# The second parts of the third mixer's weights, formed in the second feed-forward and kept in DRAM

## The chip, the core and the metric

The kernel runs on one NeuronCore of a Trainium2 chip. The metric is the device time of one execution in microseconds (us). The engines are TensorE (PE; its weight loads are PEld), VectorE (DVE), ScalarE (ACT), GpSimd (POOL) and SyncE (SP), which issues the DMAs of this kernel. Each works through its own instructions in the order in which they stand in the program, and waits on semaphores for the others.

## The reference

`x` is 512 tokens of 1024 features in float32. `first_block` is a feed-forward (SwiGLU of width 2816), a mixer (a gated linear recurrence beside a neighbourhood attention) and another feed-forward. `second_block` has two layers, each a mixer and a feed-forward with a convolution; the mixer of the second layer, the third mixer of the kernel, is the one concerned:

```python
def odd_mixer(h, w_in, w_out, w_cc, b_cc, ln_g, ln_b):
    p = h @ w_in
    a, gate, q, k, v = jnp.split(p, [...], axis=-1)
    g = a * jax.nn.sigmoid(gate)
    g = causal_dwconv(g, w_cc) + b_cc
    y_c = jax.nn.silu(layer_norm(g, ln_g, ln_b))
    y_d = stick_breaking(heads(q), heads(k), heads(v))
    return jnp.concatenate([y_c, y_d], axis=-1) @ w_out
```

`w_in` is 1024x2560 and `w_out` 1024x1024; the convolution has 31 taps over 512 channels, and the attention 8 heads of width 64.

## The kernel before

**Products in three parts.** Every float32 matrix is split into two float32r parts: `hi`, a rounded copy, and `lo = x - hi`. A product is three matmuls, hi·hi, lo·hi and hi·lo (`mm3`, lines 134 to 136). An activation is split by `split` (L128 on ACT, L129 on DVE), a weight tile by `wload`.

**Loading weights.** `wload` (L95) takes one tile of 128x1024 numbers (512 KB): a DMA from SP into one of three buffers `raw` (L104), a cast on ACT into one of three `whi` (L118), a subtraction on DVE into one of three `wlo` (L119). The three `raw` buffers are used in turn by all loads of the program; a buffer is free when its subtraction is done. `whi` and `wlo` are free when PE has used them. Some stages bring further buffers for their first loads (`bh`, `bl`), and the last projections of a mixer have `oh`, `ol`.

**Stages.** `build` goes through f1, m1, f2, e, f3, o, f4 (feed-forwards and mixers by turns). A stage's first projections are done by `begin` in two halves of 256 tokens, because the normalised activations `hh`, `hl` of the first half are there before those of the second. Ahead of the second half stands a chain on DVE, ACT and PE: the sums of squares, `rnorm` (L257 to L267), the new residual and its norm.

**The second feed-forward, f2** (`ffn`). For each of 22 `j` two projections of 24 matmuls of 512 columns, on weight tiles 2j and 2j+1, then a few operations on DVE and ACT (gate, product, split). Its 44 up tiles are the `raw<-w_ffn_gu` in the rows.

**The third mixer, o** (`odd`). It has 20 tiles of `w_in_odd` and 8 of `w_out_odd`. Generators for the projections and attention heads (`unit`, `gated`, `attend`) and for the convolution (`conv`, L1016 to L1020, 27 taps per channel group on DVE, 3 on ACT and POOL) are interleaved by `weave`. An attention head goes from PE (logits) to ACT (L970, L971), to DVE (a scan `f`, L973, and a product `b`, L974), to PE (transposes, L471), to ACT and DVE (L474, L475) and back to PE (L487).

The order of the instructions on each engine is set by the framework's scheduler when the kernel is built, and is fixed then.

Of the kernel before, what the change touches and what calls it, by code (L numbers as in the profile page):

```python
# [9 lines left out]
F32 = mybir.dt.float32  # L10
F32R = mybir.dt.float32r
AF = mybir.ActivationFunctionType
ALU = mybir.AluOpType
# [3 lines left out]
P = 128  # L17
S = 512
# [3 lines left out]
KF = DFF // P  # L22
# [9 lines left out]

HALVES = (slice(0, S // 2), slice(S // 2, S))
WHOLE = slice(0, S)


class Net:
# [56 lines left out]
    def wload(self, src, alloc=None, cuts=None):  # L94


        nc = self.nc
        n = math.prod(src.shape[1:])
        raw = self.wp.tile([P, 1024], F32, name="raw", tag="raw", bufs=3)
        if cuts is None:  # L100
            dst = raw[:, :n]
            if len(src.shape) == 3:
                dst = dst.rearrange("p (m k) -> p m k", m=src.shape[1])
            nc.sync.dma_start(dst, src)  # L104
        if alloc is None:
            his = [self.wp.tile([P, 1024], F32R, name="whi", tag="whi", bufs=3)[:, :n]]
            los = [self.wp.tile([P, 1024], F32R, name="wlo", tag="wlo", bufs=3)[:, :n]]
        else:
            his, los = alloc()
        if cuts is not None:  # L110
            his, los = ([t[:, a:b] for a, b in zip((0,) + cuts, cuts)] for t in (his[0], los[0]))
        out, c0 = [], 0
        for hi, lo in zip(his, los):
            c = slice(c0, c0 + hi.shape[1])
            if cuts is not None:
                nc.sync.dma_start(raw[:, c], src[:, c])
                self.load_x(HALVES[0], c0 // P, c.stop // P)
            nc.scalar.copy(hi, raw[:, c])  # L118
            nc.vector.tensor_tensor(out=lo, in0=raw[:, c], in1=hi.bitcast(F32), op=ALU.subtract)  # L119
            out += [(hi[:, f : f + P], lo[:, f : f + P]) for f in range(0, hi.shape[1], P)]  # L120
            c0 = c.stop
        return out

    def split(self, pool, src, tag, name="sp", bufs=None, eng=None):
        nc = self.nc
        hi = pool.tile([P, S], F32R, name=name + "h", tag=tag, bufs=bufs)
        lo = pool.tile([P, S], F32R, name=name + "l", tag=tag, bufs=bufs)
        nc.scalar.copy(hi, src)  # L128
        (eng or nc.vector).tensor_tensor(out=lo, in0=src, in1=hi.bitcast(F32), op=ALU.subtract)  # L129
        return hi, lo  # L130
# [12 lines left out]
    def proj(self, src, acts, kind="m", key=None):  # L143
# [5 lines left out]
        for k0 in range(0, K, 8):  # L149
            ks = range(k0, min(K, k0 + 8))  # L150
            w = self.wload(src[:, k0 * P : ks.stop * P])
            ks = self.order or ks
            self.mmk(ps, w, acts, ks, WHOLE, ks[0] if self.order else 0, ks[-1] if self.order else K - 1)
        return ps
# [22 lines left out]
    def finish(self, src, acts, split, evac, after, pool=None):  # L177
# [4 lines left out]
        for m in range(n):  # L182
            evac(m, self.proj(src[m], acts, "mo"[m % 2], key=("out", m)), WHOLE)
        if not split:
            return after(WHOLE)
        alloc = None
# [130 lines left out]
    def first_prep(self, spec):  # L317
# [3 lines left out]
        for k in range(KD):  # L321
            self.h_scaled(spec, k, WHOLE)
        for k in range(KD):
            self.stat(self.X[k], WHOLE, k == 0)

# [32 lines left out]
    def first_begin(self, tiles, allocs):  # L358
# [13 lines left out]
        def after():  # L372
            self.consts()
            for k in range(KD):
                self.stat(self.X[k], WHOLE, k == 0)
            self.prep(spec, WHOLE)
# [2 lines left out]
        self.begin(tiles, allocs, before, after, lambda: scaled(HALVES[0]))  # L379


    def ffn(self, up, down, nxt, conv=None, post=None):
        nc, tc = self.nc, self.tc
        with tc.tile_pool(name="mida", bufs=KD) as sa, tc.tile_pool(name="mid", bufs=2 * KF - KD) as sp:
            with tc.tile_pool(name="ft", bufs=2) as fp:
                part = lambda nm: [sp.tile([P, S], F32R, name=nm, tag="s") for _ in range(2)]
                tiles = [((up.tensor.name, i), up[i]) for i in range(6)]
                allocs = [lambda: (part("bh"), part("bl"))] * 3
                if self.early:
                    self.begin(tiles, allocs)  # L390
                else:
                    self.first_begin(tiles, allocs)
                    self.early = True
                R = self.R
                if conv is not None:
                    pads = [fp.tile([P, S + 2], F32, name=f"pad{i}", bufs=1) for i in range(2)]
                    for t in pads:
                        nc.gpsimd.memset(t[:, 0:2], 0.0)
                mids = []
                h = self.H  # L400
                for j in range(KF):
                    pg = self.proj(up[2 * j], h, "m", key=(up.tensor.name, 2 * j))
                    pu = self.proj(up[2 * j + 1], h, "o", key=(up.tensor.name, 2 * j + 1))
                    gp = fp.tile([P, S], F32, name="gp", tag="gp")
                    if conv is None:
                        nc.vector.tensor_tensor(out=gp, in0=pg, in1=R, op=ALU.mult)
                    else:
                        wn, bn, l = conv
                        pad = pads[j % 2]
                        nc.vector.tensor_tensor(out=pad[:, 2:], in0=pg, in1=R, op=ALU.mult)  # L410
                        w = lambda t: self.vec(wn, (l * 3 + t) * KF + j)
                        nc.scalar.activation(gp, pad[:, 2:], AF.Identity, bias=self.vec(bn, l * KF + j), scale=w(2))
                        nc.vector.scalar_tensor_tensor(gp, pad[:, 1 : S + 1], w(1), gp, ALU.mult, ALU.add)
                        nc.vector.scalar_tensor_tensor(gp, pad[:, 0:S], w(0), gp, ALU.mult, ALU.add)
                    nc.scalar.activation(gp, gp, AF.Silu)
                    md = fp.tile([P, S], F32, name="md", tag="md")
                    nc.vector.tensor_tensor(out=md, in0=pu, in1=gp, op=ALU.mult)  # L417
                    mids.append(self.split(sa if j < KD // 2 else sp, md, "s", "m"))
            with tc.tile_pool(name="fm", bufs=KD) as mp:
                mix = {}  # L420

                def evac(m, ps, c, last=False):
                    if post is None:
                        t = self.tmp("dx")
                        nc.vector.scalar_tensor_tensor(t[:, c], ps, 0.5, R[:, c], ALU.mult, ALU.mult)
                        nc.vector.tensor_tensor(out=self.X[m][:, c], in0=self.X[m][:, c], in1=t[:, c], op=ALU.add)
                        self.updated(nxt, m, c, last)
                    else:
                        if m not in mix:
                            mix[m] = mp.tile([P, S], F32, name="mix", tag="mix")  # L430
                        nc.vector.tensor_tensor(out=mix[m][:, c], in0=ps, in1=R[:, c], op=ALU.mult)
                        self.stat(mix[m], c, m == 0, "mix", last)

                def after(c):
                    if post is not None:
                        self.post(mix, *post, nxt, c)
                    self.prep(nxt, c)

                self.finish(down, mids, 3 if nxt[0] == "normed" else 2, evac, after)
# [676 lines left out]
def build(tc, ins, out, stages=STAGES):  # L1116
    with ExitStack() as ctx:
        n = Net(ctx, tc, ins)
        n.out = out
        n.early = stages[0] != "f1"  # L1120
        if n.early:
            n.consts()
        if n.early:
            n.first_prep(PREP[stages[0]])
            n.prep(PREP[stages[0]], WHOLE)
        for s, t in zip(stages, [*stages[1:], "end"]):
            nxt = PREP.get(t, ("end",))
            if s == "f1":
                n.ffn(ins["w_ffn1_gu"], ins["w_ffn1_down"], nxt)
            elif s == "m1":  # L1130
                n.mixer1(nxt)
            elif s == "f2":
                n.ffn(ins["w_ffn2_gu"], ins["w_ffn2_down"], nxt)
            elif s == "e":
                n.even(nxt)
            elif s == "f3":
                n.ffn(ins["w_up0"], ins["w_down0"], nxt, conv=("w_fc", "b_fc", 0), post=("norm_g", 3 * KD))
            elif s == "o":
                n.odd(nxt)
            elif s == "f4":  # L1140
                n.ffn(ins["w_up1"], ins["w_down1"], nxt, conv=("w_fc", "b_fc", 1), post=("norm_g", 7 * KD))
# [139 lines left out]
```

## Time and profile before

| | us |
|---|---|
| median of 3 runs | 2491.81 (2491.55 to 2491.85) |
| the profiled execution, its time | 2491.55 |
| its span | 2489.8 |
| PE busy | 2411.6 |
| DVE busy | 1470.8 |
| ACT busy | 1100.2 |
| mean granted clock of PE, share of full speed | 0.985 |

The span goes from the first instruction to the last and is what the rows' times count from; 1.75 us of the profiled execution's time lie around it. Busy times of one engine don't overlap with each other. A busy PE isn't one at its peak, since its matmuls are pipelined and each is shown longer than its share. In the timeline the second feed-forward's up phase goes from about 878 to 1117 us, and the third mixer from about 1829 to 2074.

### The profile page before, as it was taken

The numbers are of one execution on the slowest core, as the hardware profiler recorded it, in microseconds if no ns is written. First come the engines' busy times: TensorE is split into PE (matmuls) and PEld (weight loads), VectorE is DVE, ScalarE is ACT, GpSimd is POOL, SyncE is SP. The second block draws the span as 40 slices with busy tenths as digits, with TensorE's granted clock in tenths as the row PEclk, the third lists the DMA queues.
The fourth block names the chain that finished last, engine by engine and source line by source line (L and its number), as shares of the span: only waits on it lengthen the run. The fifth ranks groups of instructions, "written<-read, shape, count | busy, mean of one in ns | idle before, by whom it ended". The sixth has DMA issues, their size and how long they took to land.

```text
span 2489.8 us, 31983 instructions
## 1 busy us (share of the span) xinstructions
PE 2411.6 (97%) x12710; PEld 2056.2 (83%) x12710; DVE 1470.8 (59%) x2496; ACT 1100.2 (44%) x1793; POOL 39.8 (2%) x75
## 2 busy tenths in 40 slices
PE   9999999999999999999999999999998879999998
PEld 8888898777777798888987898888887759888887
DVE  5444357888888643433566665554369996655434
ACT  5222236766666532322456543333245656433322
POOL 0000000000000000000000000000001120000000
PEclk9999999999999999999999999999998989999999
DMA  4232333222322223233432322233331202223332
GB/s 149 94 101 91 95 112 124 94 80 86 99 79 91 89 89 101 94 97 94 133 107 81 106 77 68 93 102 88 117 105 61 68 26 94 68 94 100 91 95 93
DMA packets 70949, 232.03 MB, mean 93 GB/s; under 512 B 7984, under 2 KB 12720, under 8 KB 70800
## 3 DMA queue, kind: packets, MB, share of 16 engines
q1 hardware_dynamic: 70800, 229.99, 29.1%
q8 instruction: 100, 1.64, 0.3%
q14 instruction: 49, 0.40, 0.1%
HBM read 227.84 MB, written 2.12 MB: 92 GB/s over the span
## 4 chain that ended last, share of the span: by engine, by line
PE 83%; DVE 10%; ACT 4%; issue 1%; DMA 1%; POOL 0%; SPq 0%; ACTq 0%; DVEq 0%; POOLq 0%
PE psm L136 15%; PE psm L134 15%; PE psm L135 15%; PE pso L134 10%; PE pso L135 10%; PE pso L136 10%; DVE wlo L119 1%; ACT whi L118 1%; PE pst L471 1%; PE pso L487 1%; DVE pso L1018 1%; DVE f L973 1%; PE pst L136 1%; PE pst L134 1%; PE pst L135 1%
## 5 line engine op out<-in xcount | busy, mean ns | idle before, releaser
L118 ACT CAST whi<-raw 128x1024 fp32r<-128x1024 f32 (+3 forms) x402 | 408.5, 1017 | 835.0 <-issue 457.5
L119 DVE TENSOR_TENSOR wlo<-raw,whi 128x1024 fp32r<-128x1024 f32 (+3 forms) x402 | 474.8, 1182 | 312.2 <-ACT whi L118 310.8
L134 PE MATMUL psm<-hh,whi 128*128 128x512 f32 (+1 forms) x1512 | 572.0, 379 | 7.3 <-ACT hh L285 3.1
L136 PE MATMUL psm<-hl,whi 128*128 128x512 f32 (+1 forms) x1512 | 568.2, 376 | 0.1
L135 PE MATMUL psm<-hh,wlo 128*128 128x512 f32 (+1 forms) x1512 | 568.1, 376 | 0.0
L134 PEld LDWEIGHTS psm<-hh,whi 128*128 128x128 f32 x1512 | 285.0, 189 | 57.0 <-ACT hh L285 3.9
L136 PEld LDWEIGHTS psm<-hl,whi 128*128 128x128 f32 x1512 | 285.2, 189 | 50.1 <-DVE hl L286 1.1
L135 PEld LDWEIGHTS psm<-hh,wlo 128*128 128x128 f32 x1512 | 285.4, 189 | 46.4
L134 PE MATMUL pso<-hh,whi 128*128 128x512 f32 (+1 forms) x728 | 273.0, 375 | 0.9 <-ACT whi L118 0.9
L135 PE MATMUL pso<-hh,wlo 128*128 128x512 f32 (+1 forms) x728 | 272.7, 375 | 0.7 <-DVE wlo L119 0.7
L136 PE MATMUL pso<-hl,whi 128*128 128x512 f32 (+1 forms) x728 | 272.8, 375 | 0.0
L135 PE MATMUL psm<-mh,wlo 128*128 128x512 f32 (+1 forms) x506 | 172.4, 341 | 1.6 <-DVE wlo L119 1.6
L134 PE MATMUL psm<-mh,whi 128*128 128x512 f32 (+1 forms) x506 | 172.1, 340 | 0.0
L136 PE MATMUL psm<-ml,whi 128*128 128x512 f32 (+1 forms) x506 | 171.9, 340 | 0.0
L417 DVE TENSOR_TENSOR md<-pso,gp 128x512 f32<-128x512 f32 x84 | 58.1, 692 | 187.5 <-PE pso L136 186.0
L135 PEld LDWEIGHTS pso<-hh,wlo 128*128 128x128 f32 x728 | 138.2, 190 | 25.1 <-DVE wlo L119 1.0
L134 PEld LDWEIGHTS pso<-hh,whi 128*128 128x128 f32 x728 | 138.1, 190 | 24.8 <-ACT whi L118 1.1
L136 PEld LDWEIGHTS pso<-hl,whi 128*128 128x128 f32 x728 | 138.1, 190 | 24.6 <-issue 0.5
L135 PE MATMUL pso<-mh,wlo 128*128 128x256 f32 (+1 forms) x440 | 145.6, 331 | 1.3 <-DVE wlo L119 1.3
L134 PE MATMUL pso<-mh,whi 128*128 128x256 f32 (+1 forms) x440 | 145.8, 331 | 0.3 <-ACT whi L118 0.3
L136 PE MATMUL pso<-ml,whi 128*128 128x256 f32 (+1 forms) x440 | 145.7, 331 | 0.0
L135 PEld LDWEIGHTS psm<-mh,wlo 128*128 128x128 f32 x506 | 96.7, 191 | 12.8 <-DVE wlo L119 2.2
(291 smaller groups left out, 3729.9 us busy)
## 6 DMA issues: line engine op xcount, KB each, us to landing
raw<-w_up SPq DMA_DIRECT2D x88, 512.0 KB, 3.3
raw<-w_ffn_gu SPq DMA_DIRECT2D x87, 512.0 KB, 3.2
raw<-w_in SPq DMA_DIRECT2D x56, 512.0 KB, 3.3
raw<-w_ffn_down SPq DMA_DIRECT2D x40, 512.0 KB, 3.5
raw<-w_down SPq DMA_DIRECT2D x38, 512.0 KB, 3.5
raw<-w_in_even SPq DMA_DIRECT2D x24, 512.0 KB, 3.5
raw<-w_in_odd SPq DMA_DIRECT2D x20, 512.0 KB, 3.3
raw<-w_ffn_down SPq DMA_DIRECT2D x20, 384.0 KB, 3.1
```

The lines of the kernel that those rows point to most:

```text
L118: nc.scalar.copy(hi, raw[:, c])
L119: nc.vector.tensor_tensor(out=lo, in0=raw[:, c], in1=hi.bitcast(F32), op=ALU.subtract)
L134: nc.tensor.matmul(out, w[0], x[0], start=start, stop=False)
L135: nc.tensor.matmul(out, w[1], x[0], start=False, stop=False)
L136: nc.tensor.matmul(out, w[0], x[1], start=False, stop=stop)
L417: nc.vector.tensor_tensor(out=md, in0=pu, in1=gp, op=ALU.mult)
L471: nc.tensor.transpose(pt[:, i * P : (i + 1) * P], p[:, i * P : (i + 1) * P], self.ident)
L487: nc.tensor.matmul(o[:, q0:q1], V[:, g, a].rearrange("p i d -> p (i d)"), p[:, c], start=first, stop=g == 3 and p is pl, skip_group_check= ...
L973: nc.vector.tensor_tensor_scan(r, r, zero.to_broadcast([P, w]), 1.0, ALU.mult, ALU.add)
L1018: nc.vector.scalar_tensor_tensor(t, pad[:, i : i + S], w(i), t, ALU.mult, ALU.add)
```

## The change

A new class `Split` stands for a weight tensor with its second part in DRAM. `presplit` walks over the tiles of a weight: it loads one into a `raw` buffer, casts its halves to a temporary `hi` on ACT, subtracts in place on DVE, so that `raw` holds the second part, and writes `raw` to DRAM. It is a generator; `ffn` of f2 takes 28 steps of it, spread over the 22 `j` of the up phase (20 tiles of `w_in_odd`, then 8 of `w_out_odd`). `wload` of such a tensor loads the tile into `raw` and casts it to `hi` as before, and brings the second part by a DMA into `wlo`, `bl` or `ol` where the subtraction was.

```diff
--- before.py
+++ after.py
@@ -32,6 +32,19 @@
 
 HALVES = (slice(0, S // 2), slice(S // 2, S))
 WHOLE = slice(0, S)
+
+
+class Split:
+
+
+    def __init__(self, raw, lo):
+        self.raw, self.lo, self.shape = raw, lo, raw.shape
+
+    def __getitem__(self, i):
+        return Split(self.raw[i], self.lo[i])
+
+    def rearrange(self, *a, **kw):
+        return Split(self.raw.rearrange(*a, **kw), self.lo.rearrange(*a, **kw))
 
 
 class Net:
@@ -96,6 +109,7 @@
 
         nc = self.nc
         n = math.prod(src.shape[1:])
+        src, second = (src.raw, src.lo) if isinstance(src, Split) else (src, None)
         raw = self.wp.tile([P, 1024], F32, name="raw", tag="raw", bufs=3)
         if cuts is None:
             dst = raw[:, :n]
@@ -116,10 +130,32 @@
                 nc.sync.dma_start(raw[:, c], src[:, c])
                 self.load_x(HALVES[0], c0 // P, c.stop // P)
             nc.scalar.copy(hi, raw[:, c])
-            nc.vector.tensor_tensor(out=lo, in0=raw[:, c], in1=hi.bitcast(F32), op=ALU.subtract)
+            if second is not None:
+                dst = lo
+                if len(src.shape) == 3:
+                    dst = dst.rearrange("p (m k) -> p m k", m=src.shape[1])
+                nc.sync.dma_start(dst.bitcast(F32), second)
+            else:
+                nc.vector.tensor_tensor(out=lo, in0=raw[:, c], in1=hi.bitcast(F32), op=ALU.subtract)
             out += [(hi[:, f : f + P], lo[:, f : f + P]) for f in range(0, hi.shape[1], P)]
             c0 = c.stop
         return out
+
+    def presplit(self, name):
+
+        nc, src = self.nc, self.ins[name]
+        lo = self.dp.tile(list(src.shape), F32, name=name + "_lo")
+        self.ins[name] = Split(src, lo)
+        for m in range(src.shape[0]):
+            raw = self.wp.tile([P, 1024], F32, name="raw", tag="raw", bufs=3)
+            nc.sync.dma_start(raw, src[m])
+            low = raw.bitcast(F32R)
+            for c in (slice(0, S), slice(S, 2 * S)):
+                hi = self.tmp("hi", dt=F32R)
+                nc.scalar.copy(hi, raw[:, c])
+                nc.vector.tensor_tensor(out=low[:, c], in0=raw[:, c], in1=hi.bitcast(F32), op=ALU.subtract)
+            nc.sync.dma_start(lo[m], raw)
+            yield
 
     def split(self, pool, src, tag, name="sp", bufs=None, eng=None):
         nc = self.nc
@@ -379,7 +415,7 @@
         self.begin(tiles, allocs, before, after, lambda: scaled(HALVES[0]))
 
 
-    def ffn(self, up, down, nxt, conv=None, post=None):
+    def ffn(self, up, down, nxt, conv=None, post=None, extra=None):
         nc, tc = self.nc, self.tc
         with tc.tile_pool(name="mida", bufs=KD) as sa, tc.tile_pool(name="mid", bufs=2 * KF - KD) as sp:
             with tc.tile_pool(name="ft", bufs=2) as fp:
@@ -416,6 +452,10 @@
                     md = fp.tile([P, S], F32, name="md", tag="md")
                     nc.vector.tensor_tensor(out=md, in0=pu, in1=gp, op=ALU.mult)
                     mids.append(self.split(sa if j < KD // 2 else sp, md, "s", "m"))
+                    if extra is not None:
+                        gen, steps = extra
+                        for _ in range(steps * (j + 1) // KF - steps * j // KF):
+                            next(gen, None)
             with tc.tile_pool(name="fm", bufs=KD) as mp:
                 mix = {}
 
@@ -1130,7 +1170,10 @@
             elif s == "m1":
                 n.mixer1(nxt)
             elif s == "f2":
-                n.ffn(ins["w_ffn2_gu"], ins["w_ffn2_down"], nxt)
+                extra = n.chain(n.presplit("w_in_odd"), n.presplit("w_out_odd"))
+                n.ffn(ins["w_ffn2_gu"], ins["w_ffn2_down"], nxt, extra=(extra, 28))
+                for _ in extra:
+                    pass
             elif s == "e":
                 n.even(nxt)
             elif s == "f3":
```

How the instructions stand. Line numbers behind "now" are those of the changed file: L118 is the load into `raw`, L137 that of the second part, L151 and L157 the load and the write of `presplit`.

SP, in the middle of f2's up phase, now (before, these are loads `raw<-w_ffn_gu` alone, 44 in a row):

```order
L118 DMA raw<-w_ffn_gu 128x1024
L151 DMA raw<-w_in_odd 128x1024
L118 DMA raw<-w_ffn_gu 128x1024
L157 DMA w_in_odd_lo<-raw 128x1024
L118 DMA raw<-w_ffn_gu 128x1024
L151 DMA raw<-w_in_odd 128x1024 x2
L157 DMA w_in_odd_lo<-raw 128x1024
L118 DMA raw<-w_ffn_gu 128x1024
L157 DMA w_in_odd_lo<-raw 128x1024
L118 DMA raw<-w_ffn_gu 128x1024
```

Between two loads of up tiles stands now a load of a mixer's tile or a write of its second part.

SP, at the start of the third mixer, now (before, eight loads `raw<-w_in_odd` in a row follow those of `w_down`):

```order
L118 DMA raw<-w_down 128x1024 x2
L118 DMA raw<-w_down 128x768
L118 DMA raw<-w_in_odd 128x1024 x3
L137 DMA wlo<-w_in_odd_lo 128x1024 x3
L118 DMA raw<-w_in_odd 128x1024
L137 DMA bl<-w_in_odd_lo 128x1024
L118 DMA raw<-w_in_odd 128x1024
L137 DMA bl<-w_in_odd_lo 128x1024
L118 DMA raw<-w_in_odd 128x1024 x3
```

The loads of the second parts stand between the loads into `raw`: three behind the third, one behind the fourth and one behind the fifth.

DVE, at the same place, in the chain ahead of the begin's second half, before:

```order
L119 TENSOR_TENSOR wlo<-raw,whi 128x768
L225 TENSOR_TENSOR acc<-acc,sq 128x256
L119 TENSOR_TENSOR wlo<-raw,whi 128x1024 x2
L431 TENSOR_TENSOR mix<-pso,R 128x256
L257 TENSOR_SCALAR v<-pst 128x2
L119 TENSOR_TENSOR wlo<-raw,whi 128x1024
L259 RECIPROCAL r<-u 128x2
L263 SCALAR_TENSOR_TENSOR y<-r,v 128x1 x2
L119 TENSOR_TENSOR bl<-raw,bh 128x1024
L264 SCALAR_TENSOR_TENSOR r<-y,r 128x2
L119 TENSOR_TENSOR bl<-raw,bh 128x1024
L342 SCALAR_TENSOR_TENSOR mix<-mix,vecs,pst 128x256 x2
```

and now, where L295, L299 and L300 are the old L259, L263 and L264, and L378 and L380 the old L342 and L344:

```order
L139 TENSOR_TENSOR wlo<-raw,whi 128x768
L261 TENSOR_TENSOR acc<-acc,sq 128x256
L471 TENSOR_TENSOR mix<-pso,R 128x256
L293 TENSOR_SCALAR v<-pst 128x2
L295 RECIPROCAL r<-u 128x2
L299 SCALAR_TENSOR_TENSOR y<-r,v 128x1 x2
L300 SCALAR_TENSOR_TENSOR r<-y,r 128x2
L378 SCALAR_TENSOR_TENSOR mix<-mix,vecs,pst 128x256 x2
L380 TENSOR_TENSOR x<-x,mix 128x256 x2
```

The five subtractions of the begin's tiles are gone; the one of `w_down` (128x768) stays ahead.

## Rows read from the trace of the kernel before

**Rows 1.** The page's busy time of each engine, and VectorE's tenths in 40 slices

```profile
PE 2411.6 (97%) x12710; PEld 2056.2 (83%) x12710; DVE 1470.8 (59%) x2496; ACT 1100.2 (44%) x1793; POOL 39.8 (2%) x75
...
DVE  5444357888888643433566665554369996655434
```

**Rows 2.** Windows: length, busy us (x instructions) by engine, PEclk, DMA share, GB/s

```profile
931.00:1115.00 184.00, 184.00 (x814) 152.35 (x813) 75.42 (x85) 53.71 (x68) 0.00 (x0) 1.00 0.29 95
1870.00:1900.00 30.00, 30.00 (x187) 26.96 (x186) 26.25 (x37) 18.32 (x29) 6.81 (x6) 1.00 0.23 71
1900.00:2050.00 150.00, 118.08 (x544) 93.20 (x542) 146.99 (x218) 82.93 (x169) 27.60 (x47) 0.90 0.15 50
2050.00:2074.00 24.00, 23.25 (x100) 19.45 (x101) 15.17 (x25) 17.72 (x26) 1.44 (x3) 0.86 0.26 85
```

**Rows 3.** VectorE's groups from 1900 to 2050: count, busy us, mean ns, idle before

```profile
L1018 DVE SCALAR_TENSOR_TENSOR pso<-po,vecs,pso 128x512 f32<-128x512 f32 x83 | 61.4, 745 | 0.4
L973 DVE TENSOR_TENSOR_SCAN f<-f,zero 128x256 f32<-128x256 f32 (+3 forms) x31 | 30.1, 972 | 0.4 <-ACT f L970 0.2
L974 DVE TENSOR_TENSOR b<-b,f 128x256 f32<-128x256 f32 (+3 forms) x31 | 18.1, 585 | 0.1
L119 DVE TENSOR_TENSOR wlo<-raw,whi 128x1024 fp32r<-128x1024 f32 x14 | 17.0, 1215 | 0.1
```

**Rows 4.** Waits of PE from 1900 to 2050: us in total, times, longest

```profile
PE pst L471 <- DVE b L974: 19.9, 14, 3.4
PE psm L134 <- DVE kl L570: 3.4, 2, 3.0
```

**Rows 5.** The chain that ended last, 1900 to 2050, shares by line

```profile
by line: DVE pso L1018 16.4%; DVE f L973 15.7%; issue 10.7%; DVE b L974 10.3%; PE psm L135 4.8%; PE psm L136 4.5%; DVE pl L475 4.3%; PE psm L134 4.0%; DVE wlo L119 3.1%; PE pso L487 2.8%; DVE qs L557 2.8%; ACT whi L118 2.3%; DVE kl L570 2.2
```

**Rows 6.** VectorE's timeline at the mixer's start: start us, us, instruction

```profile
1840.55 0.95 DVE L119 TENSOR_TENSOR wlo<-raw,whi 128x768 fp32r<-128x768 f32 x1
...
1842.06 2.35 DVE L119 TENSOR_TENSOR wlo<-raw,whi 128x1024 fp32r<-128x1024 f32 x2
...
1846.45 1.23 DVE L119 TENSOR_TENSOR wlo<-raw,whi 128x1024 fp32r<-128x1024 f32 x1
...
1848.44 1.23 DVE L119 TENSOR_TENSOR bl<-raw,bh 128x1024 fp32r<-128x1024 f32 x1 [0.30 <-ACT bh L118]
1849.59 0.16 DVE L264 SCALAR_TENSOR_TENSOR r<-y,r 128x2 f32<-128x2 f32 x1
1849.77 1.23 DVE L119 TENSOR_TENSOR bl<-raw,bh 128x1024 fp32r<-128x1024 f32 x1
```

**Rows 7.** PE's timeline ahead of the begin's second half

```profile
1862.16 1.22 PE L267 MATMUL pst<-spread,r 128*128 128x128 f32 x4 [1.33 <-DVE r L264]
```

**Rows 8.** VectorE's groups from 911 to 1115, in the second up phase

```profile
L129 DVE TENSOR_TENSOR ml<-md,mh 128x512 fp32r<-128x512 f32 x19 | 13.0, 685 | 0.7 <-ACT mh L128 0.7
```

**Rows 9.** ScalarE's groups in the same stretch

```profile
L128 ACT CAST mh<-md 128x512 fp32r<-128x512 f32 x18 | 11.1, 617 | 0.0
```

**Rows 10.** ScalarE's timeline from 931 to 937

```profile
931.13 1.05 ACT L118 CAST whi<-raw 128x1024 fp32r<-128x1024 f32 x1 [3.90 <-issue]
...
936.57 1.05 ACT L118 CAST whi<-raw 128x1024 fp32r<-128x1024 f32 x1 [3.87 <-issue]
```

**Rows 11.** DMA from 880 to 1120: the mean rate; issues, KB, us to landing

```profile
DMA packets 6223, 22.60 MB, mean 94 GB/s; under 512 B 688, under 2 KB 688, under 8 KB 6212
...
raw<-w_ffn_gu SPq DMA_DIRECT2D x37, 512.0 KB, 3.2
```

**Rows 12.** The same from 2065 to 2080

```profile
DMA packets 856, 3.12 MB, mean 208 GB/s; under 512 B 95, under 2 KB 95, under 8 KB 856
...
raw<-w_up SPq DMA_DIRECT2D x5, 512.0 KB, 4.4
```

**Rows 13.** The same from 15 to 30

```profile
DMA packets 1680, 3.64 MB, mean 242 GB/s; under 512 B 136, under 2 KB 1035, under 8 KB 1678
...
raw<-w_ffn_gu SPq DMA_DIRECT2D x4, 512.0 KB, 5.4
```

## Prediction

> **What bounds the kernel now.** I read the page first. PE is busy for 97% of the span, so over the whole kernel only PE's gaps can be won; but VectorE (DVE) has three slices in a row at nine tenths, near 1870 to 2050 [rows 1]. The windows show why that place differs. In f2's up phase PE is busy 184 of 184 us, while DVE has 75.42 and ACT 53.71. In the third mixer it turns round: from 1900 to 2050 DVE is busy 146.99 of 150 us and PE 118.08. Just ahead, from 1870 to 1900, PE is full (30.00 of 30), and behind, from 2050 to 2074, nearly so (23.25 of 24) [rows 2]. The groups of DVE in its full stretch are convolution taps (L1018, 61.4 us), the attention's scan and product (L973, L974: 48.2) and 14 subtractions that make second parts of weights (L119: 17.0 us, 1.215 each) [rows 3]. The waits of PE name DVE: 19.9 us in 14 places for the product `b` [rows 4]. So here DVE sets the pace, and elsewhere PE does. The chain of waits warns: only 3.1% of these 150 us, 4.65 us, go through L119 itself [rows 5].
>
> **The change part by part.** The sum is made against the profiled execution, 2491.55 us (span 2489.8 and 1.75 around it); the median of the runs is 0.26 above it.
>
> *Removed.* 28 subtractions, 20 of `w_in_odd` and 8 of `w_out_odd`. Five lie in the begin, four from 1870 to 1900, 14 from 1900 to 2050, five from 2050 to 2074.
>
> The 14 are worth 17.0 us of DVE's time. At the upper end all of it comes off the stretch; at the lower end only what lies on the chain, 4.65 us. Without them DVE still needs 130.0 us there and PE 118.1, so DVE stays the longest and the upper end is the nearer. Not every gap closes: behind a faster DVE come the hand-overs between engines, 10.7% of the chain as "issue" [rows 5]. I take **14 us**, three off the upper end; that is a choice.
>
> The four ahead of 1900 (4.9 us of DVE) lie under a full PE, and I count nothing; if the taps that they push back later stand in the way, they give up to 4.9. The five behind 2050 lie beside a PE with 0.75 us of gaps: nothing, at most 0.75.
>
> *The begin.* Three of its five subtractions stand in the chain ahead of the second half, behind which PE waits [rows 7]. From the start of the first of them at 1846.45 to `r` at 1849.59 pass 3.14 us, 2.4 of them subtractions [rows 6]: up to 2.4 can be won. Against that, SP issues in order, and the loads of second parts stand behind the third load into `raw`. That one needs the buffer of the `w_down` subtraction, which ends at 1840.55 + 0.95 = 1841.5 [rows 6]. With a landing of 4.4 us, as where transfers crowd [rows 12], the first second part is there at 1845.9; now it is made by about 1843.2, halfway through the pair that starts at 1842.06 [rows 6]. That is 2.7 us late, and PE's sums of squares for the chain stand in its queue behind matmuls that use it. I take 0, between 2.4 won and 2.7 lost.
>
> *Added in f2.* 56 casts of 128x512 on ACT and 56 subtractions on DVE. Like ones take 617 ns [rows 9] and 685 ns [rows 8]: 34.6 and 38.4 us in all. Both engines have over half of the phase free beside a full PE [rows 2]: cost 0. If that cover were gone, each `j` would carry some 3.3 us more of these.
>
> *Added transfers.* 28 loads and 28 writes of 512 KB in f2, and 28 loads in the mixer in place of the subtractions. In f2 that is 29.4 MB over the up phase of some 239 us: 94 GB/s [rows 11] become about 217. Before, each load there landed in 3.2 us [rows 11]. At 208 GB/s one took 4.4 [rows 12], at 242 GB/s 5.4 [rows 13]. A write of 512 KB is not in the trace; I bound it by the same rows, 3.2 to 5.4, and take 4.4, the row at the nearest rate.
>
> What counts is the `raw` buffer. A `presplit` tile holds it for load, two casts, the last subtraction and write: 4.4 + 1.23 + 0.69 + 4.4 = 10.7 us. A projection takes 936.57 - 931.13 = 5.44 us [rows 10], one `j` 10.88. With mostly one such tile per `j` among three buffers the turn fits, barely; the six `j` with two move on to another buffer. Also an up tile's cast starts when PE frees a buffer, two projections ahead of its use: 10.88 us, less 1.05 for the cast and 1.2 for the subtraction leaves 8.6 us of lead. So I take 0 for f2, and as the other end, at 5.4 us: a turn of 12.7 us, 1.85 too long, in 19 `j` 35.2 us, less the lead 8.6: 26.6 us lost.
>
> The Trainium skill ("DMA: Bandwidth & Descriptors", "Anatomy of one DMA") puts a transfer at about 2.0 us plus its bytes at 436 GB/s, and says that the fixed part is mostly the receipt of the last write, heaviest where DRAM is the target. For 512 KB that is 3.2 us, an estimate that agrees with [rows 11]; by it a turn would be 8.3 us and f2 safe, but its remark on writes to DRAM speaks against this change, and no row here has one of this size.
>
> *In the mixer*, a second part's load waits until PE frees `wlo`, like the cast of the first part before it, and then needs 4.4 us in place of cast and subtraction, 2.3. From 1900 on 14 tiles share 150 us, over 10 each, and the lead is two tiles: hidden, 0.
>
> Sum: 2491.55 - 14 = 2477.55, **2477.5 us**.
>
> **The rivals.**
> 1. *The chain, not DVE's sum, sets the mixer.* The 14 subtractions then give what lies on the chain: 2491.55 - 4.65 = 2486.9, with the begin's 2.7 lost 2489.6. For it: the 3.1%. Against: a DVE with 3 us of gaps in 150 has hardly room for a chain that ignores it.
> 2. *The three `raw` buffers starve f2* (slower). PE is full there, so any gap is lost time. The transfers must land in over about 5.1 us: then a turn is 1.2 us too long, 19 `j` lose 22.6 less the lead of 8.6, and the mixer's 14 are gone. At 5.4 the time is 2491.55 - 14 + 26.6 = 2504.2. For it: 217 GB/s lies between rows of 4.4 and 5.4, and SP's writes wait for DVE with up tiles queued behind. Against: those rows are bursts, and f2's transfers are spread. The Trainium skill ("Perfetto Trace Analysis", "Optimization Strategy") reads a gap that repeats on the engine that should be full as a sign of too little buffer space for the next tile; by that rule such gaps would stand once per `j`. So far the trace shows none in f2, PE being full there.
> 3. *Second parts come late in the mixer*: PE waits for a DMA where it waited for DVE. If each of the 14 tiles is late by 1 us, the 14 are eaten: 2491.5, no change. Against: the lead of two tiles.
>
> That the subtractions stay can't be: the order of the instructions shows them gone.
>
> **How the numbers follow.** No change means within 0.2%, 5 us, about what a measurement of this kernel can tell. Forecast 0.62 (2468 to 2484, ends of its terms), rival 1 0.18, rival 2 0.12, rival 3 0.08. Faster: the forecast and some 0.14 of rival 1, 0.76. No change: the rest of rival 1 and of rival 3, 0.12. Slower: rival 2, 0.12. The range goes from 2468 (17.0, 4.9 and some of the begin) to 2489 (rival 1 with most of the begin's loss); rival 2, part of rival 3 and a gain beyond all terms are left out.
>
> **What would show it.** From 1900 on DVE's subtractions L119 are gone, DVE's busy time there falls by 17 us and PE's wait for `b` by about half; the mixer, from its first tile's load to its last output, is some 14 us shorter. In f2 PE stays full with its loads landing under 4.5 us, and the mixer begins when it did. I'm wrong if PE shows gaps in f2 that wait for `whi` or `wlo`, if PE waits for second parts from DRAM in the mixer, or if DVE idles there while PE waits no less.

## The result, and the profile after

The changed kernel takes 2469.48 us (median of 4 runs, 2468.92 to 2469.74) against 2491.68 us (4 runs, 2490.96 to 2491.85): a ratio of 0.9913, interval 0.9901 to 0.9925, so 22.2 us faster. The forecast was 14.3 us faster, 2477.5, in a range of 2468 to 2489, so the time lies 1.5 us inside the range's lower end. The profiled execution took 2468.92 us, its span 2467.1.

Busy time and VectorE's tenths on the changed kernel's page, beside [rows 1]:

```profile
PE 2401.1 (97%) x12710; PEld 2046.1 (83%) x12710; DVE 1474.5 (60%) x2524; ACT 1129.3 (46%) x1849; POOL 38.8 (2%) x75
...
DVE  5444347888888755553566665554358985655434
```

The same 12710 matmuls kept PE busy 10.5 us less. DVE has 28 instructions more (56 less 28), its slices in f2 rose from 3 and 4 to 5, and of its three slices at nine tenths in a row one is left.

To compare the mixers, I cut both traces at the same events: the sums `v` that open the mixer's begin, the attention's first scan, its last scan, and the sums `v` of the next stage. The windows (length, busy us by engine, PEclk, DMA share, GB/s) of the kernel before:

```profile
1828.16:1894.53 66.37, 62.49 (x440) 59.52 (x440) 52.90 (x107) 35.01 (x64) 4.53 (x8) 0.92 0.34 110
1894.53:2048.02 153.49, 123.55 (x571) 97.87 (x569) 150.48 (x226) 85.47 (x173) 30.23 (x50) 0.90 0.15 47
2048.02:2089.17 41.15, 38.42 (x219) 34.18 (x220) 23.13 (x36) 26.68 (x41) 1.44 (x3) 0.92 0.33 110
```

and of the changed kernel, with its f2 window ahead, which answers to [rows 2]:

```profile
931.00:1115.00 184.00, 184.00 (x813) 152.35 (x812) 99.36 (x127) 75.65 (x110) 0.00 (x0) 1.00 0.63 217
...
1826.21:1888.82 62.61, 60.70 (x440) 57.45 (x440) 46.67 (x103) 34.34 (x64) 4.23 (x8) 0.97 0.56 194
1888.82:2025.78 136.96, 116.12 (x571) 91.41 (x569) 132.89 (x207) 84.90 (x173) 29.55 (x50) 0.99 0.34 107
2025.78:2066.72 40.94, 38.21 (x219) 33.92 (x220) 17.37 (x32) 26.59 (x41) 1.44 (x3) 0.92 0.48 168
```

The begin, up to the first scan, is 3.76 us shorter, the stretch from first to last scan 16.53, the tail 0.21. The other 1.95 us lie ahead of the mixer, which opens at 1826.21 and not 1828.16. That is no work of the change: one of the experiments, *fill*, has the old program up to the third mixer, and its mixer opens at 1826.59, while two with the new work in f2 and a full PE there open at 1825.59 (*f2_only*) and 1827.95 (*f2_48_own*).

```profile
1826.59 0.15 DVE L259 TENSOR_SCALAR v<-pst 128x2 f32<-128x2 f32 x1
```

So some 1.6 us of such an offset is scatter between two profiled runs, and about 20.5 of the 22.7 us between the spans is the mixer's.

In the stretch DVE's busy time fell by 150.48 - 132.89 = 17.59 us, and its idle time rose from 3.01 to 4.07: 17.59 - 1.06 = 16.53. Busy and idle time add up to the window on any engine, so this sum alone shows no cause; what speaks for DVE is how little it idled, 2% of the stretch before and 3% after, while PE idled 29.9 and 20.8 us. DVE's groups there, beside [rows 3], without the subtractions:

```profile
L1058 DVE SCALAR_TENSOR_TENSOR pso<-po,vecs,pso 128x512 f32<-128x512 f32 x85 | 62.6, 744 | 0.6
L1013 DVE TENSOR_TENSOR_SCAN f<-f,zero 128x128 f32<-128x128 f32 (+3 forms) x32 | 29.9, 936 | 0.7 <-ACT f L1010 0.6
L1014 DVE TENSOR_TENSOR b<-b,f 128x128 f32<-128x128 f32 (+3 forms) x31 | 19.1, 617 | 0.4
```

PE's waits from first to last scan say something that I had not forecast. Before, beside [rows 4], these two stood there too (`acc` is a running sum of squares, `kh` and `kl` are the two parts of an attention's keys):

```profile
PE pst L471 <- ACT acc L221: 2.6, 1, 2.6
PE pst L471 <- ACT kh L571: 1.9, 1, 1.9
```

After:

```profile
PE pst L511 <- DVE b L1014: 18.2, 17, 2.8
PE psm L172 <- DVE yl L165: 0.4, 1, 0.4
```

The wait for `b` went from 19.9 to 18.2 us only. The list of before names no `wlo`: nowhere in the stretch did PE wait directly for a weight's subtraction. What PE lost are the long waits for `kl`, `acc` and `kh` (7.9 us together) and 7.4 us of its own busy time: the granted clock of the stretch rose from 0.90 to 0.99.

In f2, with 217 GB/s in place of 94, the loads and writes landed like this (beside [rows 11]):

```profile
raw<-w_ffn_gu SPq DMA_DIRECT2D x38, 512.0 KB, 3.7
w_in_odd_lo<-raw SPq DMA_DIRECT2D x20, 512.0 KB, 3.0
raw<-w_in_odd SPq DMA_DIRECT2D x18, 512.0 KB, 3.5
raw<-w_out_odd SPq DMA_DIRECT2D x8, 512.0 KB, 4.2
```

and PE was busy 184.00 of 184 us.

### The profile page after: what moved, and what is told of

The parts are those of the page before. It is cut to its first block, busy times and chain, and to the rows that moved or that the text cites. A ratio compares the mean times of both kernels' runs of the same rounds, so it can differ in the third digit from the quotient of the medians.

```text
span 2467.1 us, 32225 instructions
## 1 busy us (share of the span) xinstructions
PE 2401.1 (97%) x12710; PEld 2046.1 (83%) x12710; DVE 1474.5 (60%) x2524; ACT 1129.3 (46%) x1849; POOL 38.8 (2%) x75
## 4 chain that ended last, share of the span: by engine, by line
PE 83%; DVE 10%; ACT 5%; issue 1%; DMA 1%; POOL 0%; SPq 0%; ACTq 0%; DVEq 0%; POOLq 0%
PE psm L172 15%; PE psm L170 15%; PE psm L171 15%; PE pso L170 10%; PE pso L171 10%; PE pso L172 10%; ACT whi L132 1%; DVE wlo L139 1%; DVE pso L1058 1%; PE pst L511 1%; PE pso L527 1%; PE pst L278 1%; PE pst L170 1%; PE pst L172 1%; PE pst L171 1%
## 5 line engine op out<-in xcount | busy, mean ns | idle before, releaser
L139 DVE TENSOR_TENSOR wlo<-raw,whi 128x1024 fp32r<-128x1024 f32 (+2 forms) x380 | 447.6, 1179 | 311.1 <-ACT whi L132 309.9
```

## The experiments

Theory A: DVE's own work sets the mixer's stretch, and the clock follows. Rivals: B, PE waited for subtractions that stood late in DVE's order; C, the clock gives part of the gain by itself; and rival 2 of the prediction, the `raw` buffers, as a limit of f2. Twelve kernels ran. Ratios are against runs of the kernel before on the same chip, whose medians were 2491.28, 2489.89, 2490.10 and 2490.16 us in the four sets. Line numbers in a run's rows are those of its own file.

### The old load on DVE, with nobody waiting for it

```diff
                 nc.sync.dma_start(dst.bitcast(F32), second)
+                nc.vector.tensor_tensor(out=raw.bitcast(F32R)[:, c], in0=raw[:, c], in1=hi.bitcast(F32), op=ALU.subtract)
```

> The changed kernel, and for each of the mixer's 28 tiles the old subtraction too, written back into `raw`, where nobody reads it: DVE's load is as before the change (28 x 1.2 = 33 us more), while PE still takes the second parts from DRAM and waits for none of these subtractions. Theory A, DVE's own time sets the mixer: the 20.5 us that the mixer became shorter go back nearly whole, 2486 to 2492 us. Rival B, what was won is that PE no longer waits for a subtraction that stands late in DVE's order: the time stays at 2469 to 2474 us.

Measured: 2486.73 us, ratio 0.9982 (0.9973 to 0.9992). First to last scan:

```profile
1891.20:2043.36 152.16, 130.18 (x571) 101.66 (x569) 146.97 (x226) 86.05 (x173) 33.16 (x50) 0.88 0.29 97
```

With DVE's work back, the stretch is back at 152.16 us, although PE takes every second part from DRAM. PE's waits there name no `whi` and no `wlo`, so the added work doesn't hold PE up by way of the weights. The longest are:

```profile
PE pst L512 <- DVE b L1015: 12.8, 8, 3.9
PE psm L171 <- ACT v L1027: 3.1, 2, 1.9
```

B falls; the load on DVE is the cause. The scheduler put the work of the stretch in another order here too, but the length goes with the load and not with the order: it is 152.16 to 153.50 us in the three kernels that have the 14 subtractions, all 27 taps per group and no added matmuls (the kernel before, *f2_only*, *dve_load*), and 136.26 to 137.59 in the six that have the taps and no subtraction there. The whole kernel is 4.5 us short of the old time, 1.3 of it in the stretch and 1.3 in the begin. The clock went back too, to 0.88, and PE's busy time grew by 14 us for the same matmuls.

### f2's work alone, and the mixer without the loads

*f2_only* (the mixer's tensors are set back to the plain ones):

```diff
             elif s == "o":
+                for k in ("w_in_odd", "w_out_odd"):
+                    ins[k] = ins[k].raw
                 n.odd(nxt)
```

> f2 forms and writes the second parts, but the mixer subtracts as before and nobody reads what was written: the cost of the added work alone. If f2 hides it (prediction): 2490 to 2493 us. If three `raw` buffers starve f2 by even a part: over 2495, with gaps of PE between 880 and 1117.

Measured: 2489.59 us, ratio 0.9995 (0.9986 to 1.0004), and a stretch as long as before:

```profile
1891.40:2044.90 153.50, 123.64 (x571) 97.88 (x569) 150.49 (x225) 85.41 (x173) 30.17 (x50) 0.90 0.14 47
```

The 56 casts, 56 subtractions and 56 transfers cost nothing that can be measured.

*no_lo*:

```diff
-                dst = lo
...
-                nc.sync.dma_start(dst.bitcast(F32), second)
+                lo = hi
```

> The changed kernel without the 28 loads of second parts in the mixer: the first part stands for the second in the matmuls, so that the second part of the mixer's weights is left out of the computation. f2 still forms and writes them. If the loads are hidden (my prediction): 2467 to 2471 us. If second parts come late somewhere (rival 3, or the begin's first tile): 2460 to 2467, and the wait that goes is named by PE's waits.

Measured: 2471.06 us, ratio 0.9919 (0.9903 to 0.9936); first to last scan 136.71 us. Without the loads nothing is won, so they are hidden; PE's waits in the changed kernel's stretch, above, name no DMA either. Rival 3 falls.

### The begin's five subtractions back

```diff
+            w_raw = w_in.raw
...
-                [(("gate", 0), w_in[4]), (("a", 0), w_in[0]), ...
+                [(("gate", 0), w_raw[4]), (("a", 0), w_raw[0]), ...
```

> The changed kernel, but the five tiles of the mixer's begin are subtracted as before; the other 23 come from DRAM. The changed kernel's begin was shorter by 2.8 us up to the second half's first `hl` and 0.9 more by the first scan. If the subtractions ahead of the second half's chain did that: 2472 to 2474 us and the second half's `r` some 2 to 2.5 us later against the chain's start. If the begin gained by chance of order: 2469 to 2470.

Measured: 2472.90 us, ratio 0.9924 (0.9910 to 0.9939), 3.4 us over the changed kernel by the medians and 2.7 by the ratios, whose intervals overlap. Opening to first scan, and first to last scan:

```profile
1827.51:1893.57 66.06, 61.95 (x440) 58.60 (x441) 52.26 (x107) 34.78 (x64) 4.23 (x8) 0.95 0.42 144
1893.57:2029.83 136.26, 115.96 (x571) 91.59 (x569) 132.78 (x206) 85.07 (x173) 29.60 (x50) 0.99 0.33 108
```

The begin is back at 66 us and the stretch keeps its gain. Among the kernels the begin scatters: it takes 62.3 to 64.6 us in the eight traces without subtractions in it (*hi_lo*, which loads otherwise, left out) and 65.0 to 66.4 in the five with them. So the direction is clear, and the size is known to some 2 us only. DVE's timeline of the second half's chain, first here and then in the changed kernel:

```profile
1845.48 0.16 DVE L293 TENSOR_SCALAR v<-pst 128x2 f32<-128x2 f32 x1 [1.59 <-PE pst L278]
1845.59 1.23 DVE L139 TENSOR_TENSOR wlo<-raw,whi 128x1024 fp32r<-128x1024 f32 x1
...
1848.16 1.23 DVE L139 TENSOR_TENSOR bl<-raw,bh 128x1024 fp32r<-128x1024 f32 x1 [0.88 <-ACT bh L132]
1849.30 0.15 DVE L300 SCALAR_TENSOR_TENSOR r<-y,r 128x2 f32<-128x2 f32 x1
```

```profile
1844.43 0.16 DVE L293 TENSOR_SCALAR v<-pst 128x2 f32<-128x2 f32 x1 [2.08 <-PE pst L278]
...
1845.51 0.16 DVE L300 SCALAR_TENSOR_TENSOR r<-y,r 128x2 f32<-128x2 f32 x1
```

From `v` to `r` 3.82 us with two subtractions between, 1.08 without.

### The clock alone

*fill* is the kernel before with four matmuls (`FILL = 4`) ahead of each group of transposes:

```diff
                 pt = self.psum("t")
+                if mask is not None:
+                    for _ in range(FILL):
+                        nc.tensor.matmul(pt[:, :n], Q[a][:, 0:P], K[a][0][:, 0:n], start=True, stop=True)
```

> The kernel before, with four more matmuls ahead of each of the 32 groups of transposes in the third mixer's attention; their result is written over by the transposes. PE has something to do while it waits for `b`, some 17 us of it, and DVE's work is unchanged. It tells whether the higher granted clock of the mixer (0.90 before the change, 0.99 after it, first scan to last) is a cause of the gain. Theory A, DVE's time sets the stretch and the clock only follows: the clock rises and the time stays within 3 us of the kernel before, 2488 to 2494 us. Theory C, the clock gives part of the gain by itself: 2480 to 2486 us.

Measured: 2503.48 us, ratio 1.0057 (1.0040 to 1.0074), outside what either theory gave:

```profile
1893.00:2060.34 167.34, 142.75 (x687) 114.90 (x686) 153.75 (x225) 85.00 (x172) 31.00 (x50) 0.92 0.13 45
```

This run doesn't decide on the clock, since it rose to 0.92 only. It shows another thing: of 19.2 us more on PE 13.85 reached the end, and DVE idled 13.6 us. PE's and DVE's queues hand over to each other 32 times; half of these times PE doesn't wait (16 waits for `b` here), and there its own time can count. On the clock one window of the kernel before says more:

```profile
1910.00:1924.00 14.00, 7.90 (x24) 5.94 (x25) 13.90 (x22) 3.94 (x8) 0.30 (x3) 0.51 0.07 19
```

Where the clock was lowest (0.51, nearly all of the time at 1.2 GHz), PE was idle for 6.1 of 14 us, and DVE busy for 13.90: a faster PE had nothing to win there. Over the whole stretch DVE's 3.01 us of idle time bound what a faster PE alone could have won before. That doesn't bound what the changed kernel would lose if the clock had stayed at 0.90: at *fill*'s share, 13.85 of 19.2, the 7.4 us of PE's time that came back would be some 5.4 of the 16.53 us, an estimate. So the load on DVE starts the gain, but how much of it comes by way of the clock was shown by no run.

### How far f2's buffers reach

*f2_48* forms w_in_odd twice, 48 tiles in place of 28; *f2_48_own* gives these tiles two buffers of their own:

```diff
-            raw = self.wp.tile([P, 1024], F32, name="raw", tag="raw", bufs=3)
+            raw = self.pr.tile([P, 1024], F32, name="praw", tag="praw", bufs=2)
```

> The changed kernel with 48 tiles formed and written in f2 in place of 28 (the 20 of w_in_odd twice, the first time for nobody): over two for each `j`, where the rival of the starved `raw` buffers would show first. By the holds that the changed kernel's landings give, 3.5 + 1.2 + 0.7 + 3.0 = 8.4 us for such a tile and some 6 for an up tile, a `j` needs 2.2 x 8.4 + 2 x 6 = 30.3 us of buffer time, and three buffers give 32.6. If that sum is what counts: 2469 to 2473 us, PE without gaps in f2. If landings rise over 4.5 us at some 310 GB/s: 2475 to 2520 us, with gaps between 880 and 1117.

> The kernel with 48 tiles formed in f2, but these have two buffers of their own, so that the up tiles have the three `raw` buffers to themselves; the bytes moved and the order of issue on SP are nearly the same. The shared-buffer kernel lost 20 us, PE waiting for the cast `whi` behind late loads. If the turn of the shared buffers did it (rival 2's mechanism): 2469 to 2474 us, no gaps of PE in f2. If the traffic of 280 GB/s or SP's queue did it: 2480 to 2495.

Measured: 2491.95 us shared (ratio 1.0006, 0.9997 to 1.0016), which gives back all of the gain, and 2471.68 with own buffers (0.9924, 0.9909 to 0.9938). The windows from 880 to 1117, shared:

```profile
880.00:1117.00 237.00, 229.34 (x1104) 192.86 (x1103) 141.37 (x190) 115.63 (x171) 0.00 (x0) 0.99 0.79 282
```

PE's waits there:

```profile
PE psm L170 <- ACT whi L132: 5.9, 2, 3.3
PE psm L171 <- DVE wlo L139: 1.8, 3, 0.8
```

and its landings:

```profile
raw<-w_in_odd SPq DMA_DIRECT2D x38, 512.0 KB, 4.6
w_in_odd_lo<-raw SPq DMA_DIRECT2D x40, 512.0 KB, 2.9
raw<-w_ffn_gu SPq DMA_DIRECT2D x38, 512.0 KB, 3.5
```

With own buffers, the window and two of the landings:

```profile
880.00:1117.00 237.00, 236.73 (x1151) 199.56 (x1151) 141.85 (x195) 114.94 (x173) 0.00 (x0) 1.00 0.80 286
...
praw<-w_in_odd SPq DMA_DIRECT2D x38, 512.0 KB, 4.8
raw<-w_ffn_gu SPq DMA_DIRECT2D x37, 512.0 KB, 5.1
```

At the same rate of transfers (282 and 286 GB/s) the gaps are there with shared buffers and nearly gone with own ones: the turn of `raw` makes them, not the traffic, and with own buffers even slower landings do no harm. My sum of 30.3 us took the changed kernel's landings. With its own (4.6 + 1.2 + 0.7 + 2.9 = 9.4 us for such a tile) a `j` needs 2.2 x 9.4 + 2 x 6 = 32.7 us of the 32.6 that three buffers give: they are full, so the landings that I put in failed and not the sum. It also leaves out the time that an up tile waits in `raw` for a free `whi`. With shared buffers the mixer opens at 1846.06, 19.9 us after the changed kernel's. Some 12 us of that are PE idle between 860 and 1280 us; the granted clock fell there too, to 0.92 from 1117 to 1160, and the rest is not told apart. The Trainium skill ("Perfetto Trace Analysis", "Optimization Strategy") says that repeated gaps on the engine that should be full can mean too little buffer space for the next tile; these two runs agree.

### Less work for DVE still

Three ways to take 6 or 12 us more from DVE: two of its 27 taps per channel group left out (*less_taps*), or 5 or 7 taps in place of 3 on ACT and POOL (*nt5*, *nt7*), the former also with the tap's copy in a shared temporary (*nt5_tmp*).

```diff
-                        else:
+                        elif i not in (7, 22):
                             nc.vector.scalar_tensor_tensor(t, pad[:, i : i + S], w(i), t, ALU.mult, ALU.add)
```

```diff
-            NT = 3
+            NT = 5
```

> The changed kernel with 2 of the 27 taps that each channel group has on DVE left out of the convolution: 8 operations, 8 x 0.745 = 6.0 us of DVE less, and no work put on another engine. Theory A, DVE's own time sets the stretch still: first scan to last falls from 137.0 to about 131.4 us and the kernel to 2463 to 2465. Rival D, PE's and ACT's queues are next, as in the runs with 5 and 7 taps on ACT and POOL, where DVE idled 18 us and more: 2467 to 2483.

> The changed kernel with 5 of the 30 inner taps of each channel group on ACT and POOL in place of 3: 8 fewer taps on DVE, 8 x 0.746 = 6.0 us. Theory A: the stretch from first scan to last falls by 0.94 of that, as in the change (16.5 for 17.6), and the kernel to 2463 to 2465 us. Rival: POOL's additions, 1.3 us each in a chain, or the hand-overs are next: 2467 to 2472.

> As the run with 5 taps, with 7 of 30: 16 fewer taps on DVE, 11.9 us. Theory A, as long as DVE is the longest (118 us of DVE against 116 of PE from first scan to last): 2457 to 2461 us. Past the point where PE or the chain of the attention takes over: 2461 to 2466, and less won than twice what 5 taps give.

> The changed kernel with 5 taps on ACT and POOL, as before, but the scaled copy of a tap goes to one of three temporaries and not to the single buffer `tap`, so that ACT needs not wait for POOL's addition (9.0 us of waits in the run with the single buffer). If this wait in ACT's order held up the attention's `f` and `qs`: 2463 to 2468 us. If it is the order on ACT and PE that the scheduler chose: 2475 to 2484.

Measured: *less_taps* 2473.54 us (ratio 0.9942, 0.9924 to 0.9959), *nt5* 2482.96 (0.9965), *nt7* 2484.13 (0.9978), *nt5_tmp* 2478.82 (0.9955): all slower than the changed kernel, where A said faster. First to last scan of *less_taps* and of *nt5*:

```profile
1888.38:2029.13 140.75, 117.16 (x571) 93.75 (x569) 128.45 (x198) 84.36 (x173) 30.88 (x50) 0.96 0.31 104
```

```profile
1891.15:2040.21 149.06, 122.51 (x571) 98.43 (x569) 130.84 (x198) 88.64 (x179) 38.47 (x56) 0.92 0.29 98
```

The stretch is longer than the changed kernel's 136.96, in *nt7* 151.88 and in *nt5_tmp* 146.08 us. DVE's busy time fell by 4.4 us in *less_taps* and 2.1 in *nt5*, not by the 6.0 taken off, and it now idles 12.3 and 18.2 us. Its longest waits in *less_taps*:

```profile
DVE f L1013 <- ACT f L1010: 3.2, 4, 2.1
DVE qs L597 <- ACT qs L596: 3.1, 4, 1.4
```

Where it is lost, the windows from the last tap on show, of the changed kernel and of *less_taps*:

```profile
2011.30:2025.78 14.48, 9.15 (x46) 6.17 (x45) 13.92 (x21) 9.28 (x22) 7.14 (x9) 1.00 0.00 0
```

```profile
2008.40:2029.13 20.73, 12.86 (x52) 9.47 (x52) 15.74 (x23) 10.79 (x26) 9.28 (x11) 0.84 0.00 0
```

Up to the last tap *less_taps* is 2.5 us shorter (120.0 and 122.5); behind it only the attention's hand-overs are left, and there it loses 6.25, with the clock at 0.84 in place of 1.00. The scheduler also put DVE's and PE's work in another order, so how much is the shorter work and how much the order is not told apart. The copy in one of three temporaries took 3 to 4 us off *nt5*, but the intervals of the two ratios overlap (0.9952 to 0.9978 and 0.9940 to 0.9969): that ACT's wait for POOL was a part of that loss is likely, not shown.

### First parts from DRAM too

In *hi_lo*, f2 also writes the rounded parts, and the mixer loads both without a cast:

```diff
-            nc.scalar.copy(hi, raw[:, c])
...
+                for dst, part in ((hi, src), (lo, second)):
...
+                    nc.sync.dma_start(dst.bitcast(F32), part)
```

> The changed kernel, and the first parts too are written in f2 (from two buffers of their own) and loaded by the mixer: 28 casts of 1.05 us leave ACT there, 14 of them between first and last scan, and a first part needs no cast after its load. If ACT's queue is what now holds the attention's hand-overs (DVE idles 4 us for ACT and PE waits 18 us for `b`, whose product stands behind ACT's sigmoids): the stretch falls from 137 to 130 to 134 us, the kernel to 2462 to 2467. If the chain PE, ACT, DVE, PE of the attention sets it with ACT mostly waiting for PE (24.4 us for the transposes): 2467 to 2471. If f2 does not hide 28 more writes (some 280 GB/s): over 2472, with gaps of PE between 880 and 1117.

Measured: 2475.47 us, ratio 0.9940 (0.9927 to 0.9954), slower than the changed kernel:

```profile
1894.81:2031.19 136.38, 115.96 (x571) 91.30 (x569) 133.17 (x207) 72.46 (x159) 29.98 (x50) 0.99 0.31 107
```

12.4 us less on ACT shorten the stretch by 0.6: ACT's work is not what is next. The loss lies ahead: the mixer opens 3.0 us later than the changed kernel's, and its begin is 3.0 us longer. f2 has gaps again:

```profile
880.00:1117.00 237.00, 235.92 (x1155) 199.82 (x1154) 125.44 (x164) 98.87 (x141) 0.00 (x0) 1.00 0.79 278
```

In the begin a first part can't be loaded ahead into `raw`, and PE waits 1.3 us for its DMA. These waits cover some 2.4 of the 6 us; the rest is not traced, and the mixers' openings scatter by some 2 us. No version tried beats the changed kernel.

## Why the prediction was right, and where its steps were off

- **Where DVE sets the pace** [rows 1 to 4]: right. *dve_load* gives the stretch its old length back by DVE's load, and DVE idled 3.01 us of it before and 4.07 after. What part of the gain the clock carried is open.
- **"I take 14 us, three off the upper end"**: mis-sized. The stretch gave 16.53 of DVE's 17.59. I had let the 10.7% of "issue" in [rows 5] speak for new hand-over gaps; DVE's idle time grew by 1.06 us only. The chain's 3.1% for the subtractions [rows 5] was no measure: it counts those that stood on one path, while each of the 14 pushed back all that came behind it on a full engine. So rival 1 falls. The four subtractions ahead of 1900 and the five behind 2050 were taken at nothing, rightly as far as the scatter lets one tell: with the begin's five back, *begin_sub* is 0.31 us below the old begin, in which the four lie, and the tail is 0.21 shorter.
- **"The begin: I take 0"**: mis-sized, 3.76 us won between these two traces, of which *begin_sub* gives back some 3. The chain's 2.4 us [rows 6] came: from `v`, whose row of before stands below, to `r` 3.25 us before and 1.08 after, so 2.17. The 2.7 lost didn't: SP issued the first second part's load at 1836.97, not behind the subtraction that I had it wait for, and it landed some 4.2 us later, ahead of PE's first use at 1841.7. The rest was traced to no wait; PE's busy time here fell by 1.8 us, at a granted clock of 0.97 and not 0.92, and the begin's scatter is as large.

```profile
1846.34 0.16 DVE L257 TENSOR_SCALAR v<-pst 128x2 f32<-128x2 f32 x1 [1.59 <-PE pst L242]
```

SP's loads at the mixer's start, after:

```profile
1827.56 9.37 SPq L118 DMA_DIRECT2D raw<-w_in_odd  x3
1836.97 5.14 SPq L137 DMA_DIRECT2D wlo<-w_in_odd_lo  x3
```

- **f2 at 0**: right (*f2_only*), and with more room than I had worked out: a tile's turn is 3.5 + 1.23 + 0.69 + 3.0 = 8.4 us, not 10.7, since the load took 3.5 us and the write 3.0, where I had 4.4 for each. The Trainium skill ("DMA: Bandwidth & Descriptors", "Anatomy of one DMA") gives 3.2 us for 512 KB by its fit, an estimate, and the fit is one for DMAs that GpSimd issues, where these go out from SP; the measured writes lie near it. The extra weight that the section gives to a write into DRAM doesn't show in the changed kernel (writes 3.0, loads 3.5 and 4.2); in *hi_lo* three of four groups of writes (5.0 to 6.1 us) took longer than the loads (4.5 to 4.8).
- **Rival 2** names a true mechanism with its point of decision elsewhere: 28 tiles leave PE full and 48 don't. With 48, more turns and landings of 4.6 us for the mixer's tiles fill the three buffers together, well under the 5.1 us that I had asked of 28 tiles.
- **The mixer's loads at 0** and rival 3: right about the loads (*no_lo*).
- **"PE's wait for `b` by about half"**: wrong. It fell by 1.7 us. PE's gain came as other waits and as a faster clock, neither of which stood in my sum; the time came out inside the range because the sum was made on DVE.

## What to carry to other kernels

Where one engine is busy nearly all of a stretch, work taken off it is worth nearly its full time (here 16.5 of 17.6 us), whichever chain it stands on, as long as its idle time stays small; compare that engine's busy and idle time between the same two events before and after, and put its work back with nobody waiting for it to see whether the time returns. Expect the next limit right behind it: here the same kind of relief, tried once more, won nothing, since the engine then waited for the others; how much of that was the scheduler's new order stayed open. And a tile that is loaded, worked on and written back holds its buffer two transfers long: give such a stream buffers of its own before its turn fills the shared ones.

## What was not expected of the hardware

- The granted clock of PE moved when another engine's load was changed: 0.90 in the stretch before, 0.99 after, 0.88 in *dve_load*. It doesn't follow that load alone, since *nt5*, with less of it than the changed kernel, has 0.92. The same 571 matmuls took 123.55, 116.12 and 130.18 us of busy time.
- A write of 512 KB to DRAM landed in 3.0 us beside loads of 3.5 at 217 GB/s; at 278 GB/s in *hi_lo* writes took 4.3 to 6.1 and loads 4.5 to 4.8. It is not the rate alone: at 282 GB/s in *f2_48* writes took 2.9 and 3.4.
